# A two-block fp32 model on one core: norm sums and spread at fixed places among the products, weight casts behind that chain, modulation steps behind their place, first weights freed sooner

## The chip, the cores and the metric

The kernel runs on one core of a Trainium2 chip. The metric is the device time of one execution in microseconds; lower is better. The engines are called PE (TensorE, matrix products), DVE (VectorE), ACT (ScalarE), POOL (GpSimd) and SP (SyncE, which issues the DMAs). PEld is PE's own loading of stationary operands, which runs beside its products.

## The reference, cut to what matters

A sequence of 256 tokens `x` and 256 context tokens `ctx`, width 1024, go through a first block of two layers, and `x` then through a second block of two mixers. Only the first block is touched by the change. One of its layers reads, cut:

```
mod = silu(c) @ w_ada[li] + b_ada[li]          # six vectors of 1024: shift, scale, gate, twice
h = rms_norm(x, norm1_w) * (1 + sc1) + sh1
p = h @ w_in[li]                               # attention, a gated recurrence and a Fourier mix follow
x = x + g1 * (concat(att, rec, four) @ w_out[li])
h = rms_norm(x, norm2_w) * (1 + sc2) + sh2
u = conv3(h @ w_up[li])
x = x + g2 * ((silu(gate) * val) @ w_down[li])
# the same for ctx; in the second layer ctx only feeds the keys, the values and the states
```

`rms_norm` divides each token by the root of its mean square, so a layer's first product can't start before the last value of `x` of the step before has been added and squared.

## The kernel before, in words

`x` lies in SBUF as 8 tiles of 128 rows (the width) by 512 columns: columns 0 to 255 are the tokens (v = 0), 256 to 511 the context (v = 1). A product of fp32 operands is made of three: each operand is split into a high part (fp32r) and a low part, and high·high, high·low and low·high are added up in one bank of PSUM. The weights are read from HBM in pieces of 512 KB (`raw`, three buffers, issued by SP); ACT casts the high part `wH` (L136), DVE subtracts it for the low part `wL` (L138); `wH` and `wL` have two buffers each, so a third weight's casts wait until the first one's products are through.

Stages in order, with their place in the span: layer 0 (0 to 353 us, 512 columns, its last 15 us the output products in two halves of 256), its ffn (`w_up` from 356, `w_down` to 765; called FFN0 here), layer 1 (766 to 976, where the context goes only through a part of the products), its ffn (977 to 1185, 256 columns, FFN1), then the second block.

Where one stage follows another stands a **chain**, once for each half v that goes on: the last `add` to `x` (DVE, L733 in a layer, L934 in an ffn); its square on ACT (L200) and the sum `acc` of the squares (L201); `sums`, two products of `acc` with ones (L206); the root on ACT (L212); the reciprocal (L214) and two diagonals `dg` (L223) on DVE; `spread`, two products with ones (L224), which give 1/rms in all rows. Then the modulated input of the next products: for tiles k = 0 and 1 `norm_modulate` (`y` on DVE L422, high part on ACT L423, low part on DVE L424), for k = 2 to 7 `norm` (DVE, L396) and `modulate` (high part ACT L408, `y` POOL L410, low part DVE L411).

A scheduler puts each engine's instructions in order when the kernel is built, by priorities and its own estimate of times; within an engine the order is then fixed, and an instruction that waits holds up all behind it. `urgent` raises a priority; `issue_after(ins)` holds an instruction until `ins` is issued in that estimate. `rstd` is the chain before from sums to spread. `wload(..., hold=...)` holds the casts of a weight's two halves. `gemm` and `gemms` issue the products and count ticks; after so many ticks (`beside`) one step of `ada_steps` is issued: two DMAs of `w_ada` (`araw`, three buffers) and four products (L337) that work out the next modulation vectors, in layer 0 beside the products and in FFN0.

## Time and profile before

| | us |
|---|---|
| median of 3 runs | 1767.48 |
| lowest, highest | 1767.39, 1772.09 |
| the profiled execution's own time | 1768.71 |
| its span in the profile | 1766.8 |
| mean granted clock of TensorE | 0.989 |

The profile shows one execution. A row of a timeline gives the start in us, the busy time in us, engine, line, operation, the tiles out<-in, the shape, the count, and in brackets how long the engine had stood idle before it and who released it. A row of the windows gives the stretch, its length, for each engine its busy time with the count of instructions, then the granted clock of TensorE (1.00 is 2.4 GHz, 0.50 is 1.2 GHz) and the share and rate of the DMA engines. A row of the chain of waits gives start, length and what the end of the stretch stood on at that time.

### The profile page before, as it was taken

The page shows a single profiled execution, that of the slowest core. Times are in us where ns is not written, and L with a number is a line of the kernel's source. Part 1 is how long each engine was busy: PE and PEld are TensorE (multiplying, and loading weights), DVE is VectorE, ACT ScalarE, POOL GpSimd, SP SyncE. Part 2 cuts the span into 40 slices and gives each one's busy share as a digit, 9 for nine tenths or more (in the row PEclk, how much of TensorE's full clock was granted, in tenths as well). Part 3 has the DMA queues.
Part 4 walks back from the last instruction along what each step waited for, and adds up shares of the span by engine and source line. Part 5 has one row for each costly group of instructions (what it writes and reads, how often), then busy time and mean ns, then how long its engine had stood idle before and what let it go on. Part 6 is the DMA issues. An engine that isn't in the chain of part 4 may idle for free.

```text
span 1766.8 us, 29276 instructions
## 1 busy us (share of the span) xinstructions
PE 1703.3 (96%) x11646; PEld 1456.3 (82%) x11646; DVE 1018.9 (58%) x1832; ACT 843.6 (48%) x1476; POOL 312.2 (18%) x402
## 2 busy tenths in 40 slices
PE   6999899999999999989998899999999999999998
PEld 3666676887777777878787899999999999899987
DVE  4445756564433444356866666767666754645656
ACT  3435645453322433334655554665444565555543
POOL 1322210121100011125320210122201202121220
PEclk9999999999999999999999899999999999999999
DMA  9664110334445453223133446555555555444441
GB/s 328 219 202 152 45 54 25 97 129 147 146 162 182 145 189 130 86 72 108 69 97 105 141 155 205 174 175 189 183 180 187 180 179 167 154 139 148 151 144 44
DMA packets 86705, 255.45 MB, mean 145 GB/s; under 512 B 8823, under 2 KB 20471, under 8 KB 86568
## 3 DMA queue, kind: packets, MB, share of 16 engines
q1 hardware_dynamic: 86568, 253.58, 43.4%
q8 instruction: 91, 1.49, 0.3%
q14 instruction: 46, 0.38, 0.1%
HBM read 252.42 MB, written 1.13 MB: 144 GB/s over the span
## 4 chain that ended last, share of the span: by engine, by line
PE 88%; DVE 5%; ACT 4%; issue 1%; DMA 1%; POOL 1%; SPq 0%; ACTq 0%; DVEq 0%; POOLq 0%
PE pg L158 34%; PE ps L158 14%; PE pu L158 7%; PE ph L158 7%; PE pg L184 7%; PE pa L337 3%; PE pg L172 2%; PE ps L1227 2%; PE ph L499 1%; PE ps L172 1%; PE pa L1257 1%; DVE wL L138 1%; PE ps L774 1%; ACT wH L136 1%; PE ph L1253 1%
## 5 line engine op out<-in xcount | busy, mean ns | idle before, releaser
L138 DVE TENSOR_TENSOR wL<-raw,wH 128x1024 fp32r<-128x1024 f32 (+2 forms) x388 | 444.4, 1176 | 219.1 <-ACT wH L136 216.5
L136 ACT CAST wH<-raw 128x1024 fp32r<-128x1024 f32 (+2 forms) x388 | 370.5, 994 | 374.2 <-PE pg L158 149.5
L158 PE MATMUL pg<-hx,wH 128*128 128x256 f32 x1152 | 215.0, 284 | 0.0
L158 PE MATMUL pg<-hm,wH 128*128 128x512 f32 (+1 forms) x672 | 181.1, 356 | 4.6 <-DVE x L733 4.3
L158 PEld LDWEIGHTS pg<-hx,wH 128*128 128x128 f32 x1152 | 178.6, 189 | 5.3 <-issue 4.0
L158 PE MATMUL pg<-hx,wL 128*128 128x256 f32 x576 | 163.1, 283 | 0.0
L158 PEld LDWEIGHTS pg<-hm,wH 128*128 128x128 f32 x672 | 115.8, 190 | 34.6 <-issue 10.2
L926 POOL TENSOR_TENSOR tt<-tt 128x512 f32<-128x512 f32 (+1 forms) x44 | 45.0, 1022 | 451.5 <-DVE tt L923 451.5
L158 PE MATMUL pg<-hm,wL 128*128 128x512 f32 (+1 forms) x336 | 118.4, 352 | 0.0
L158 PEld LDWEIGHTS pg<-hx,wL 128*128 128x128 f32 x576 | 108.2, 188 | 0.7 <-issue 0.2
L158 PE MATMUL pg<-h,wH 128*128 128x512 f32 (+1 forms) x416 | 105.0, 342 | 0.5 <-ACT wH L136 0.5
L158 PE MATMUL ps<-h,wH 128*128 128x512 f32 (+1 forms) x416 | 104.1, 340 | 0.0
L158 PEld LDWEIGHTS pg<-h,wH 128*128 128x128 f32 x416 | 70.7, 190 | 18.4 <-ACT wH L136 8.3
L158 PE MATMUL pg<-hid,wH 128*128 128x256 f32 (+1 forms) x360 | 81.9, 319 | 1.1 <-ACT wH L136 1.1
L158 PEld LDWEIGHTS ps<-h,wH 128*128 128x128 f32 x416 | 71.4, 190 | 10.8 <-ACT bt L974 0.8
L158 PE MATMUL ps<-hid,wH 128*128 128x256 f32 (+1 forms) x344 | 77.8, 319 | 0.0
L184 PE MATMUL pg<-wH,hm 128*128 128x256 f32 x384 | 72.9, 285 | 1.2 <-ACT wH L136 1.2
L201 POOL TENSOR_TENSOR acc<-acc,y 128x256 f32<-128x256 f32 x40 | 36.9, 933 | 197.9 <-ACT y L200 197.3
L158 PEld LDWEIGHTS pg<-hm,wL 128*128 128x128 f32 x336 | 63.8, 190 | 9.7 <-issue 1.0
L158 PE MATMUL ps<-h,wL 128*128 128x512 f32 (+1 forms) x208 | 70.8, 340 | 0.5 <-DVE wL L138 0.5
L158 PE MATMUL pg<-h,wL 128*128 128x512 f32 (+1 forms) x208 | 70.7, 340 | 0.5 <-DVE wL L138 0.5
L184 PE MATMUL pg<-wH,hx 128*128 128x256 f32 x384 | 71.1, 280 | 0.0
(453 smaller groups left out, 3955.0 us busy)
## 6 DMA issues: line engine op xcount, KB each, us to landing
raw<-in_w_up_dram SPq DMA_DIRECT2D x88, 512.0 KB, 4.9
araw<-in_w_ada_dram SPq DMA_DIRECT2D x80, 512.0 KB, 4.6
raw<-in_attn_w_in_dram SPq DMA_DIRECT2D x80, 512.0 KB, 4.6
raw<-in_conv_w_in_dram SPq DMA_DIRECT2D x64, 512.0 KB, 4.6
raw<-in_w_in_dram SPq DMA_DIRECT2D x48, 512.0 KB, 4.7
raw<-in_w_down_dram SPq DMA_DIRECT2D x32, 384.0 KB, 3.7
raw<-in_w_down_dram SPq DMA_DIRECT2D x32, 320.0 KB, 3.1
raw<-in_conv_w_out_dram SPq DMA_DIRECT2D x16, 512.0 KB, 4.6
```

Of the source, the lines that this page charges most:

```text
L136: nc.scalar.copy(H[:, a:b], raw)
L138: nc.vector.tensor_tensor(L[:, a:b], raw, H[:, a:b].bitcast(F32), OP.subtract)
L158: nc.tensor.matmul(pt, a[:, k, c0:c0 + P], c[:, t0:t0 + T], start=n == 0, stop=n == tot - 1)
L172: nc.tensor.matmul(pt, a[:, k, c0:c0 + P], c[:, ts], start=k == 0 and n == 0, stop=k == last and n == 2)
L184: nc.tensor.matmul(pt[:, p0:p0 + 256], c[:, t0:t0 + P], a[:, k, :], start=n == 0, stop=n == tot - 1)
L201: st["last"] = i, (nc.vector if last else nc.gpsimd).tensor_tensor(st["acc"], st["acc"], sq, OP.add)
L337: nc.tensor.matmul(pa[32 * g:32 * g + 32, :], self.csil[:, k, :], raw[g // 2][:, g % 2], start=k == 0, stop=k == KD - 1)
L499: nc.tensor.matmul(pt[:, v, c:c + P], l, m, start=True, stop=True)
L774: nc.tensor.matmul(pts[i][:, :n], qa[h][rr, qt * P:(qt + 1) * P], kT[h][rr, k0 * P:k0 * P + n], start=True, stop=True)
L926: nc.gpsimd.tensor_tensor(tt[1], tt[0], tt[1], OP.mult)
L1227: nc.tensor.matmul(ps[v][:, o:o + ks.stop - ks.start], qh[g][rr[v], i, qs], kh[g][rr[v], i, ks], start=True, stop=True)
L1253: nc.tensor.transpose(pt[:, v, k * P:(k + 1) * P], lts[v][:, k * P:(k + 1) * P], self.ident)
```

## The change

All matrix products go through one function, `product`, which counts them. `in_products(n, f)` calls `f` after n more products. `rstd` is replaced by `chain(st, bank, n)`: it issues the sums after n[0] products and the spread after n[1], each held behind the product before it, and the next product is held behind them. The sums and the spread of one chain now share a bank (columns 256 and 257, and 0 to 255). The places are 20 and 40 products into the second half of `w_out` (for FFN0's v = 1), 12 and 30 products into FFN0's first products (v = 0), 20 and 46 into the last products of `w_down` (layer 1's v = 1), 12 and 30 into layer 1's first (v = 0). At the start of layer 0 and of FFN1 the chain has no number.

The casts of the first weights of layer 1 (`w_in` 8) are held behind the root and the diagonals of v = 1's chain, those of the second (`w_in` 6) behind the high and the low part of v = 0's tile k = 1, those of FFN0's `w_up` 1 (second half) and FFN1's `w_up` 1 (both halves) behind the chain of v = 0. The low parts of k = 6 and 7 of v = 1 are held behind v = 0's diagonals. The products of an `ada` step are held behind the last product issued. The first products of layer 0 now go through k = 0 to 3 for all four groups, then k = 4 to 7 for the first weight's two groups, then for the second's; in layer 1 and in both ffns the first weight's groups come ahead of the second's in the same way. `gemms` counts no ticks any more. `bias_rows` (10 products for the second block) moves from FFN0 to FFN1.

The diff, cut to its core:

```diff
+    def product(self, pt, a, b, start, stop):
+        with self.after(self.first):
+            self.mm = self.nc.tensor.matmul(pt, a, b, start=start, stop=stop)
+        self.first = None
+        self.done += 1
+        while self.plan and self.plan[0][0] <= self.done:
+            self.plan.pop(0)[1]()
+
+    def in_products(self, n, f):
+        self.plan.append((self.done + n, f))
...
-    def rstd(self, st):
-        pn = self.pg()
-        self.sums(pn, 0, st["acc"].rearrange("p (j t) -> p j t", j=2))
-        return self.spread(self.inv("rs", pn[:, 0:2]))
+    def chain(self, st, bank, n=None):
...
+        def sums():
+            st["pt"] = pt = bank()
+            with self.urgent(), self.after(self.mm if n else None):
+                mm = self.sums(pt, 256, st["acc"].rearrange("p (j t) -> p j t", j=2))
+            if n:
+                self.first = mm
+            with self.urgent():
+                st["r"] = self.inv("rs", pt[:, 256:258])
...
+                st["ends"] = self.root, i
...
+        for i, f in enumerate((sums, spread)):
+            if n:
+                self.in_products(n[i], f)
+            else:
+                f()
...
-            for g in range(4):
-                nc.tensor.matmul(pa[32 * g:32 * g + 32, :], self.csil[:, k, :], raw[g // 2][:, g % 2],
-                                 start=k == 0, stop=k == KD - 1)
+            with self.after(self.mm):
+                for g in range(4):
+                    nc.tensor.matmul(pa[32 * g:32 * g + 32, :], self.csil[:, k, :], raw[g // 2][:, g % 2],
+                                     start=k == 0, stop=k == KD - 1)
...
-            first = [(self.wload(d["w_in"][li, 8]),), None]
...
-                if v:
-                    first[1] = (self.wload(d["w_in"][li, 6], hold=((None, None), (None, last))),)
+            self.chain(states[0], lambda: self.psum("pu"), (12, 30))
+            first = [(self.wload(d["w_in"][li, 8], hold=(states[1]["ends"],) * 2),), None]
...
-                self.gemms(groups, acts)
+                if li == 0:
+                    groups = [(first[i // 2][0], i % 2 * P, 0, pts[i]) for i in range(4)]
+                    self.gemms(groups, acts, 0, 4)
+                    self.gemms(groups[:2], acts, 4)
+                    self.gemms(groups[2:], acts, 4)
+                else:
+                    for s in (1, 0):
+                        for k in (0, 4):
+                            modulated(s, k)
+                            if s == k == 0:
+                                w = self.wload(d["w_in"][li, 6], hold=(first[1],) * 2)
...
+            if v:
+                self.chain(st2[1], lambda: self.psum("pa"), (20, 40))
...
+        if ns == 2:
+            self.chain(st2[0], lambda: self.psum("pu"), (12, 30))
...
+            pre.append(self.wload(d["w_up"][li, 1], hold=((None, None), st2[0]["ends"])))
...
+        else:
+            self.chain(st2[0], lambda: self.psum("pu"))
+            pre.append(self.wload(d["w_up"][li, 1], hold=(st2[0]["ends"],) * 2))
...
+                    if v:
+                        self.chain(st1[1], lambda: self.psum("pa"), (20, 46))
```

What it does to the order of the instructions, at three places. The first is PE in layer 0's first products, at k = 4 (`hm_154` and on); before, `pg_472` and `ps_475` are banks of the first and second weight, and the L337 rows are a modulation step:

```order
L172 MATMUL pg_473<-hm_154,wH_237 128x512
L172 MATMUL ps_474<-hm_154,wH_239 128x512
L172 MATMUL ps_475<-hm_154,wH_239 128x512
L337 MATMUL pa_624<-araw_625,csil_77 32x512 x2
L337 MATMUL pa_624<-araw_626,csil_77 32x512 x2
L172 MATMUL pg_472<-hm_155,wH_237 128x512
L172 MATMUL pg_472<-hm_154,wL_238 128x512
```

And now (the banks are `pg_470` to `ps_473`):

```order
L152 MATMUL pg_471<-hm_154,wH_237 128x512
L152 MATMUL ps_472<-hm_154,wH_239 128x512
L152 MATMUL ps_473<-hm_154,wH_239 128x512
L152 MATMUL pg_470<-hm_155,wH_237 128x512
L152 MATMUL pg_470<-hm_154,wL_238 128x512
L152 MATMUL pg_471<-hm_155,wH_237 128x512
```

The step is gone from between the products; the first one now stands some 80 rows later, inside the value products that follow.

The second is PE at the entry to layer 1, from the last product of `w_down` on (`hid`, before):

```order
L158 MATMUL ph_6139<-hid_5687,wL_6016 128x256
L224 MATMUL pg_6217<-dg_6216,ca_71 128x128 x2
L206 MATMUL pg_6222<-ca_71,acc_5740 128x1 x2
L224 MATMUL pg_6230<-dg_6229,ca_71 128x128
L172 MATMUL pg_6331<-hm_6193,wH_6235 128x256
L172 MATMUL pg_6331<-hm_6194,wH_6235 128x256
```

Now the spread of v = 1 (L261) stands among the products of `w_down`:

```order
L152 MATMUL ps_6072<-hid_5659,wH_5976 128x256
L152 MATMUL ps_6072<-hid_5658,wL_5977 128x256
L261 MATMUL pa_6093<-dg_6100,ca_71 128x128 x2
L152 MATMUL pg_6120<-hid_5156,wH_5986 128x256
L152 MATMUL pg_6120<-hid_5155,wL_5987 128x256
```

Before, v = 0's sums and half its spread stood ahead of the first product of layer 1; now they stand behind its first 12 and 30.

The third is DVE at the same entry, from v = 1's reciprocal on; before (`wL_6236` is `w_in` 8, `wL_6284` the first half of `w_in` 6):

```order
L138 TENSOR_TENSOR wL_6236<-raw_6237,wH_6235 128x1024
L138 TENSOR_TENSOR wL_6236<-raw_6241,wH_6235 128x1024
L201 TENSOR_TENSOR acc_5740<-acc_5740,y_6136 128x256
L214 RECIPROCAL rs_6214<-sd_6212 128x2
L223 TENSOR_SCALAR dg_6216<-ca_71,rs_6214 128x128 x2
L934 SCALAR_TENSOR_TENSOR x_80<-ph_6139,mod0_162,x_80 128x256
L422 SCALAR_TENSOR_TENSOR y_6245<-x_80,A1b_5691,pg_6217 128x256
L138 TENSOR_TENSOR wL_6284<-raw_6285,wH_6283 128x1024
L201 TENSOR_TENSOR acc_5740<-acc_5740,y_6174 128x256
L424 SCALAR_TENSOR_TENSOR hm_6194<-y_6245,mod1_3657,hm_6193 128x256
```

and now (`wL_6192` is `w_in` 8):

```order
L226 RECIPROCAL rs_6098<-sd_6096 128x2
L254 TENSOR_SCALAR dg_6100<-ca_71,rs_6098 128x128 x2
L996 SCALAR_TENSOR_TENSOR x_80<-ps_6072,mod0_162,x_80 128x256
L139 TENSOR_TENSOR wL_6192<-raw_6193,wH_6191 128x1024
L139 TENSOR_TENSOR wL_6192<-raw_6197,wH_6191 128x1024
L212 TENSOR_TENSOR acc_5711<-acc_5711,y_6117 128x256
L996 SCALAR_TENSOR_TENSOR x_80<-pg_6120,mod0_162,x_80 128x256
L463 SCALAR_TENSOR_TENSOR y_6205<-x_80,A1b_5662,pa_6093 128x256
```

The two casts of `w_in` 8 have moved from ahead of the reciprocal to behind the diagonals, still ahead of `y`; those of `w_in` 6 (not shown) to behind v = 0's first two low parts.

## Rows read from the trace of the kernel before

**Rows 1.** The page, busy time, share of the span and instructions, PE.

```profile
PE 1703.3 (96%) x11646; PEld 1456.3 (82%) x11646; DVE 1018.9 (58%) x1832; ACT 843.6 (48%) x1476; POOL 312.2 (18%) x402
```

**Rows 2.** Windows: layer 1's entry, FFN1's entry; granted clock behind POOL's column.

```profile
770.00:776.50 6.50, 3.26 (x15) 3.29 (x16) 4.99 (x13) 3.65 (x8) 4.38 (x6) 0.50 0.13 51
...
982.00:988.50 6.50, 5.50 (x25) 5.21 (x25) 4.60 (x10) 3.59 (x8) 4.17 (x6) 0.52 0.04 16
```

**Rows 3.** Timeline of PE, layer 0's first products (columns as told above).

```profile
52.71 3.28 PE L337 MATMUL pa<-araw,csil 128*32 128x512 f32 x8
...
66.60 1.91 PE L337 MATMUL pa<-araw,csil 128*32 128x512 f32 x12
68.44 0.39 PE L184 MATMUL pg<-wH,hm 128*128 128x256 f32 x1
```

**Rows 4.** Timeline of DVE, the casts behind layer 0's first products.

```profile
66.78 2.36 DVE L138 TENSOR_TENSOR wL<-raw,wH 128x1024 fp32r<-128x1024 f32 x2 [0.91 <-ACT wH L136]
```

**Rows 5.** Timeline of ACT: a wait early in layer 0, a table load later.

```profile
27.09 0.37 ACT L372 COPY araw<-pa 128x256 f32<-128x256 f32 x1 [6.42 <-PE pa L317]
...
1190.81 1.28 ACT L1017 ACT_TABLE_LOAD   x1
1192.10 0.20 ACT L1017 ACTIVATE sd<-m 128x2 f32<-128x2 f32 x1
```

**Rows 6.** Timeline of PE, FFN0's entry and its third weight.

```profile
358.68 0.58 PE L172 MATMUL ph<-h,wH 128*128 128x256 f32 x1 [0.89 <-DVE h L424]
...
386.43 0.50 PE L158 MATMUL ps<-h,wL 128*128 128x512 f32 x1 [0.46 <-DVE wL L138]
```

**Rows 7.** The chain of waits through layer 1's entry.

```profile
763.48 4.44 DMA raw<-in_w_in_dram
...
772.67 4.11 POOL y L410 x5
...
777.15 1.22 DVE wL L138
...
781.09 3.67 PE pg L172 x29
```

**Rows 8.** Timeline of ACT, layer 1's entry.

```profile
761.15 2.00 ACT L136 CAST wH<-raw 128x1024 fp32r<-128x1024 f32 x2 [2.55 <-PE pu L158]
...
763.37 0.24 ACT L212 ACTIVATE sd<-pg,eps 128x2 f32<-128x2 f32 x1
```

**Rows 9.** Timeline of PE, layer 1's entry, then its third weight.

```profile
765.42 0.67 PE L224 MATMUL pg<-dg,ca 128*128 128x128 f32 x4
...
773.24 0.77 PE L224 MATMUL pg<-dg,ca 128*128 128x128 f32 x2 [4.44 <-DVE dg L223]
...
796.33 0.38 PE L184 MATMUL pg<-wH,hm 128*128 128x256 f32 x1 [1.17 <-ACT wH L136]
797.59 0.38 PE L184 MATMUL pg<-wL,hm 128*128 128x256 f32 x1 [0.88 <-DVE wL L138]
```

**Rows 10.** Timeline of DVE, layer 1's entry.

```profile
766.12 0.48 DVE L422 SCALAR_TENSOR_TENSOR y<-x,A1b,pg 128x256 f32<-128x256 f32 x1
766.58 1.23 DVE L138 TENSOR_TENSOR wL<-raw,wH 128x1024 fp32r<-128x1024 f32 x1
```

**Rows 11.** Timeline of PE, FFN1's entry and its third weight.

```profile
979.84 1.22 PE L224 MATMUL ps<-dg,ca 128*128 128x128 f32 x4 [1.39 <-DVE dg L223]
...
984.22 0.58 PE L172 MATMUL pg<-h,wH 128*128 128x256 f32 x1 [0.82 <-DVE h L424]
...
997.81 0.50 PE L158 MATMUL pg<-h,wH 128*128 128x256 f32 x2 [0.52 <-ACT wH L136]
999.07 0.38 PE L158 MATMUL pg<-h,wL 128*128 128x256 f32 x1 [0.52 <-DVE wL L138]
```

**Rows 12.** Timeline of DVE, FFN1's entry.

```profile
978.16 1.23 DVE L138 TENSOR_TENSOR wL<-raw,wH 128x1024 fp32r<-128x1024 f32 x1 [0.51 <-ACT wH L136]
...
981.10 0.87 DVE L422 SCALAR_TENSOR_TENSOR y<-x,A,ps 128x256 f32<-128x256 f32 x2 [1.12 <-PE ps L224]
```

More of the change, by code (lines that the diff above doesn't have):

```diff
@@ L64 @@
     rush = True
+    done, mm, plan, first = 0, None, [], None
     def ring(self, tag, shape, dtype=F32):
@@ L157, in gemm @@
             for a, c in ((H, h), (H, l), (L, h)):
-                nc.tensor.matmul(pt, a[:, k, c0:c0 + P], c[:, t0:t0 + T], start=n == 0, stop=n == tot - 1)
+                self.product(pt, a[:, k, c0:c0 + P], c[:, t0:t0 + T], n == 0, n == tot - 1)
                 n += 1
@@ L161, in gemm, with gemms @@
         return pt
-    def gemms(self, groups, acts):
+    def gemms(self, groups, acts, k0=0, k1=KD):
         nc = self.nc
         last = len(acts) - 1
-        for k, (h, l) in enumerate(acts):
+        for k in range(k0, k1):
+            h, l = acts[k]
             for (H, L), c0, t0, pt in groups:
@@ L171, in gemms @@
                 for n, (a, c) in enumerate(((H, h), (H, l), (L, h))):
-                    nc.tensor.matmul(pt, a[:, k, c0:c0 + P], c[:, ts], start=k == 0 and n == 0,
-                                     stop=k == last and n == 2)
-        for _ in groups:
-            self.tick()
+                    self.product(pt, a[:, k, c0:c0 + P], c[:, ts], k == 0 and n == 0, k == last and n == 2)
     def gemm_nat(self, W, acts, t0, pt, p0):
@@ L211, in inv @@
         sd = self.sml("sd", [P, 2])
-        nc.scalar.activation(sd, src, AF.Sqrt, bias=self.eps, scale=1.0 / 1024)
+        self.root = nc.scalar.activation(sd, src, AF.Sqrt, bias=self.eps, scale=1.0 / 1024)
         rs = self.sml(name, [P, 2])
@@ L225, in spread @@
         return pb
-    def rstd(self, st):
-        pn = self.pg()
-        self.sums(pn, 0, st["acc"].rearrange("p (j t) -> p j t", j=2))
-        return self.spread(self.inv("rs", pn[:, 0:2]))
+    def chain(self, st, bank, n=None):
+        nc = self.nc
+        def sums():
[6 more added lines that the diff above has]
+                st["r"] = self.inv("rs", pt[:, 256:258])
+                st["dg"] = dg = self.sml("dg", [P, 2, P], bufs=1)
+                for j in range(2):
+                    i = nc.vector.tensor_scalar(dg[:, j], self.ident, st["r"][:, j:j + 1], None, op0=OP.mult)
+                st["ends"] = self.root, i
+        def spread():
+            st["pb"] = st["pt"][:, 0:256]
+            with self.urgent(), self.after(self.mm if n else None):
+                for j in range(2):
+                    mm = nc.tensor.matmul(st["pb"][:, j * P:(j + 1) * P], self.ones, st["dg"][:, j],
+                                          start=True, stop=True)
+            if n:
+                self.first = mm
+        for i, f in enumerate((sums, spread)):
+            if n:
+                self.in_products(n[i], f)
+            else:
+                f()
     def setup(self, es):
@@ L410, in modulate @@
                 nc.gpsimd.tensor_scalar(y, n[:, i], a, b, op0=OP.mult, op1=OP.add)
-                last = nc.vector.tensor_tensor(L, y, H.bitcast(F32), OP.subtract)
+                with self.after(hold):
+                    last = nc.vector.tensor_tensor(L, y, H.bitcast(F32), OP.subtract)
         return last
@@ L585, in layer @@
                 self.wpart(*w, 4, 8)
-        pb = [None] * 2
-        for v in (1, 0):
-            with self.urgent():
-                pb[v] = self.rstd(states[v])[:, 0:256]
+        if li == 0:
+            self.chain(states[1], lambda: self.psum("pu"))
+            self.chain(states[0], lambda: self.psum2()[:, 0])
         tags = ["on", "on", "aT", "ks", "qh", "sg", "tot"]
```

77 lines of the change are left out of this document (42 added, 35 removed).

## The prediction, made before the changed kernel had run

> **What bounds the kernel now.** I read the page first. PE is busy for 96% of the span, by the profile's modelled ends [rows 1], so almost everywhere the products are the time and no reordering of other engines can gain. What can be gained lies where PE stands. The windows show where: PE is fully packed inside the ffns and the second block, and the loose stretches are the entries from one stage to the next. I then read these on PE, DVE and ACT together, at four places: layer 0's first products, FFN0's entry, layer 1's, FFN1's. Each is followed, some 12 to 30 us later, by a second short stand, the **join**, where the third weight is needed and its casts have only just begun, because the two buffers of weights come free with the last of the first products.
>
> The reader is to see two things. At layer 1's entry PE's queue is the obstacle: v = 0's spread stands in it ahead of the first product of v = 1, and waits 4.44 us for diagonals that DVE makes behind other work [rows 9]. And every stand costs twice, since the granted clock has fallen to 0.50 there, in 770 to 776.5 as in 982 to 988.5 [rows 2]: a 256-column product takes 0.213 us start to start instead of 0.118.
>
> **The change part by part.** Gains are positive.
>
> *Layer 0's first products.* A modulation step of eight rows stands at 52.71 between the products and takes 3.28 us; the twelve at 66.60 take 1.91, 0.159 each [rows 3]. So eight need 1.27, and 2.0 us of the 3.28 is a wait for the step's DMA. The new order has neither piece: the products end 3.28 earlier, at 63.3. The value products then wait for their weight. Its casts begin 3.28 earlier too, and about 0.5 more because the first weight's groups are evicted sooner: the first low part, which started at 66.78 and is half of 2.36 [rows 4], is there at 64.2, and the values start at about 64.4 instead of 68.44 [rows 3], 4.0 earlier. The twenty step rows have still to be done, inside PE's work: 20 × 0.159 = 3.2. If all of it is exposed 0.8 is left; if all falls in waits, 4.0; if one step waits 2.0 for its data again, −1.2. I take **1.4**, near the exposed end, since PE as a whole has only 4% of waits to hide them in [rows 1].
>
> *FFN0's entry.* v = 1's spread now stands 8 products ahead of the end of `w_out`, 0.95 earlier. But on DVE a cast (1.23, the duration in [rows 10]) and two sums of squares now stand ahead of `y`, so `y` comes at about 355.6 and the first low part at 358.2 to 358.6; before, PE ran on from 358.68 [rows 6]. v = 0's sums, until now done while PE stood, move among the products and cost 0.36. Net **0** (−0.5 to 0.9).
>
> *FFN0's join.* The third weight's product at 386.43 waits for a low part [rows 6], 0.86 from the start of the one before it where 0.23 is normal. The first weight's groups now end 24 to 48 products sooner and its buffer with them, so the casts lie beside products: **0.6** (0 to 1.1).
>
> *Layer 1's entry.* Before: ACT's root of v = 1 stood behind two weight casts of 2.00 and ran at 763.37 [rows 8]; the spread ran at 765.42, the first product came behind the two rows of v = 0's spread, at 773.66 [rows 9], then half clock, then a second stand for v = 0, and the last of these products started at 794.89, 1.44 before the 796.33 of [rows 9], and ended at 795.0. Now, walked along the new order: v = 1's sums at 761.1, the root at once, the spread at 762.95, among the products. These end at 765.8, 0.36 later, for v = 1's spread is among them. The casts of `w_in` 8 wait for a buffer until 762.95 and run on ACT to 765.0; their two low parts (2.36, [rows 4]) and two adds stand on DVE ahead of `y`, which comes at 767.5 instead of 766.12 [rows 10]. So this part of the chain gets **later** by 1.4. But PE's queue is free: first product 768.35, first low part 770.2, then one tile per 0.82, POOL's pace (4.11 for five, [rows 7]), so that v = 1's products end at about 778.5. v = 0's spread stands behind the 30th of them, at 776.5; its first low part comes at 780, where PE went on with v = 0 from 781.09 [rows 7]. Behind it the 48 products of v = 0 and the 48 of `w_in` 6 are free to mix: 96 × 0.118 = 11.3, end at 791.3, against 795.0. Gain **3.7**. Bounds: the two low parts of `w_in` 6 now stand on DVE ahead of v = 0's third tile (before, one of them, 1.22, stood at 777.15 ahead of its first [rows 7]); if the mixing doesn't cover them, 1.4 is lost again: 2.3. If the clock is back at full as soon as the low parts flow, 5.5.
>
> *Layer 1's join.* Two stands, 1.44 and 1.26 from start to start before the products at 796.33 and 797.59 [rows 9]; less two products of 0.118, 2.46 lost. Now the groups of `w_in` 8 end 19 products, 2.2 us, before the rest, and the third weight's casts start that much sooner: **1.9** (0 to 2.46).
>
> *FFN1's entry.* One half only, so no numbers: sums at 977.7 as before. The root no longer stands behind two casts, which brings the spread from 979.84 [rows 11] to 979.1. One cast, which stood ahead of the reciprocal at 978.16 [rows 12], now stands ahead of `y`, which comes at 980.75 instead of 981.10; the weight's second cast, 1.2, which came after all low parts, now stands ahead of the first of them. So that low part comes at 984.6 to 984.95, where PE ran on from 984.22 [rows 11]: **−0.7** (−1.5 to 0.8).
>
> *FFN1's join.* Stands of 0.79 and 0.80 before the products at 997.81 and 999.07 [rows 11], 1.35 lost; the first weight's groups end 36 products (4.2 us) sooner: **1.35** (0.7 to 1.35).
>
> *Edits at nothing.* `bias_rows` moves from one packed ffn to another. The same products, squares and casts are issued in all. Two table loads are added on ACT, 1.28 each [rows 5]: the first falls early in layer 0, into a wait of 6.42 us [rows 5], the second into layer 0's attention, where PE's work covers ACT; without that cover 1.3.
>
> On these loads a row and a rule differ: in [rows 5] the load at 1190.81 takes 1.28 and the next activation starts 0.01 us behind it. The Trainium skill, in "ScalarE: Activation LUTs", section "What ACT_TABLE_LOAD costs", adds a drain and comes to about 2.66 us for each switch. By the page an uncovered load would cost 2.66 and the forecast would be 2.66 later than the sum; the row is used.
>
> Sum: 1.4 + 0 + 0.6 + 3.7 + 1.9 − 0.7 + 1.35 = 8.25. The profiled execution took 1768.71, 1.2 above the median; from it 1760.5, and from the median 1767.48 − 8.25 = **1759.2**. A measurement of this kernel tells about 0.3% from no change, which is 5.3 us; 8.25 is above that, by little.
>
> **The rivals.**
>
> *The casts eat it.* For: at all three entries a cast has moved from ahead of the diagonals to between them and the first low part, and DVE, not PE, would then be the bound. Against: at layer 1 PE's own queue waited, and that is gone for certain. With 2.3 at layer 1, −1.5 at FFN1's entry, 1.35 at its join and nothing else, 2.1 is gained: 1765.3.
>
> *The chain does not get shorter at all.* That is, sums and spread are earlier but the first product isn't, because it waits for DVE as before. Then the joins alone pay, 0.6 + 1.9 + 1.35, and layer 0 its 1.4: 5.25, or 1762.2, on the bound of what can be told. Against: the order has the wait of 4.44 out of PE's way.
>
> *All of it comes, and the clock with it.* With shorter stands the granted clock does not fall, or is sooner back: 4.0 + 0.9 + 1.1 + 5.5 + 2.46 + 0.8 + 1.35 = 16.1, 1751.4. Against: at each entry PE still stands for two to three us by my walk, and over stands of such length it fell to 0.50 [rows 2].
>
> *Slower: the pinned steps.* A modulation step is now held behind a given product. PE takes its queue in order, so a step whose `araw` hasn't landed holds up all products behind it, as the one at 52.71 did for 2.0 [rows 3]. Layer 0 has some 15 steps, and SP now issues some of the raw weights ahead of `araw`. Five of them standing 2.0 each eat the gain of 8.25; from seven on (14) the kernel is slower by over 5.3. With ten, 1767.48 − 8.25 + 20 = 1779. Against: one step in this trace stands that long, not several.
>
> **How the numbers follow.** The forecast as walked 0.56, the casts eat it 0.20, only joins 0.06, all of it 0.10, pinned steps 0.08. Faster by over 0.3%: nine tenths of the forecast (its bounds, 4 to 13 gained, reach a little under 5.3), half of the joins alone, and all of it: 0.51 + 0.03 + 0.10 = 0.64. Within 0.3%: 0.05 + 0.20 + 0.03 = 0.28. Slower 0.08. The range leaves out half of the largest gain and the pinned steps with a little of the casts' case: 1752.5 to 1768.
>
> **What would show it.** In the trace after: at layer 1's entry no wait of several us on the spread, a first product near 768.4 and an end of the first products near 791; at the joins of layer 1 and FFN1 stands under 0.5; at FFN1's entry a first low part **later** against the sums than before, by about 0.5; in layer 0 no L377 between the first products. I am wrong if the step rows stand long again, with a wait on the `araw` DMA, or if the first product of layer 1 comes no sooner than the 773.66 of before.

## The result

The changed kernel took 1776.95 us (median of 5 runs, 1772.34 to 1779.82), the kernel before 1767.39 beside it: a ratio of 1.0051, 95% interval 1.0029 to 1.0073. It is slower by about 9 us where 8 us less were forecast. The profiled execution took 1776.95 with a span of 1774.9. The page of the changed kernel, the line that answers to [rows 1]:

```profile
PE 1709.4 (96%) x11646; PEld 1461.2 (82%) x11646; DVE 1019.8 (57%) x1832; ACT 846.7 (48%) x1478; POOL 310.8 (18%) x402
```

The page doesn't say where the time went: the same work, the same shares. A **ledger** does. Both kernels issue the same 9234 products (by `product`, or L158, L172 and L184 before) in nearly the same order. So I numbered them in order of start in each trace and took, for the n-th, its start in one kernel less its start in the other, both counted from the first product. (Before that first product the code is bound by the first DMAs; it came at 31.07 us in the profiled run of before and at 26.9 to 30.6 us in all others, also in b1 below, which is the kernel before up to there. That is run to run and belongs to no edit.) Where the difference changes, a stretch has gained or lost:

| products | stretch | predicted loss | measured loss, us |
|---|---|---|---|
| 0 to 900 | layer 0 | −1.4 | +9.24 |
| 900 to 1100 | FFN0's entry | 0 | +1.42 |
| 1100 to 1300 | its join, and bias_rows gone from there (predicted at 0) | −0.6 | −3.94 |
| 2600 to 2840 | layer 1's entry | −3.7 | −2.16 |
| 2840 to 2858 | its join | −1.9 | −1.52 |
| 3600 to 3756 | FFN1's entry | +0.7 | −0.16 |
| 3756 to 3780 | its join | −1.35 | −1.54 |
| 3855 to 3880 | bias_rows in FFN1 | 0 | +5.04 |
| 5318 to 5500 | start of the second block | 0 | +3.86 |
| all | | −8.25 | +10.35 |

Everywhere else the two run in step to 0.1 us. The six entries and joins on which the change was argued came out within 1.6 us of the prediction each (FFN0's join without `bias_rows`, see the end), and together they gain. Nearly all of the loss lies in three stretches of which the prediction said one gain and two zeros.

A ledger is read from one trace of each kernel, and traces differ. The runs of the experiments below tell by how much: where two of them run the same code with PE's rows in the same order, a difference between them belongs to no edit. The changed kernel, e2 and e3 share layer 0's order and end it at +9.24, +8.47 and +10.37; the seven runs that share e1's end it at −2.74 to −7.18. Between products 96 and 440 the three stand at +8.16 to +8.17 and the seven at −2.88 to −4.14, so that stretch is firm; the rest of layer 0 scatters. Layer 1's entry gains 1.59 to 3.38 in the ten traces that have its code, FFN1's lies between −0.64 and +1.40 in nine. FFN0's first product and the joins of layer 1 and FFN1 agree to 0.03. Where a cause is found for such a difference, below, it is a stretch in which one trace has a granted clock of 0.50 and the other 1.00.

**Layer 0.** PE of the changed kernel, the modulation steps in the value products and scores behind the first products, in order of time:

```profile
70.36 1.07 PE L377 MATMUL pa<-araw,csil 128*32 128x512 f32 x8
74.35 1.05 PE L377 MATMUL pa<-araw,csil 128*32 128x512 f32 x4
77.28 1.05 PE L377 MATMUL pa<-araw,csil 128*32 128x512 f32 x4
...
164.95 1.04 PE L377 MATMUL pa<-araw,csil 128*32 128x512 f32 x2
166.29 1.06 PE L377 MATMUL pa<-araw,csil 128*32 128x512 f32 x6
```

A step is eight rows. A piece of it takes 1.04 to 1.07 us whether it holds 8, 6, 4 or 2 rows, and 1.18 to 1.40 from the last product before it to the first behind it. In the changed kernel nearly every step up to 104 us is cut in two, and each half pays in full: 14 pieces for the first 64 rows, where the kernel before has 9. No piece stands for its DMA. The price was to be read in the kernel before too, where four rows and eight take the same:

```profile
77.12 1.05 PE L337 MATMUL pa<-araw,csil 128*32 128x512 f32 x4
...
81.09 1.07 PE L337 MATMUL pa<-araw,csil 128*32 128x512 f32 x8
```

**bias_rows in FFN1.** PE, then ACT, of the changed kernel, then the window behind the stand:

```profile
1009.45 0.60 PE L1038 MATMUL ps<-bt,rb 33*16 33x256 f32 x2
...
1010.33 0.59 PE L1038 MATMUL pu<-bt,rb 33*16 33x256 f32 x2
...
1011.19 0.59 PE L1038 MATMUL ph<-bt,rb 33*16 33x256 f32 x2
1012.81 0.53 PE L152 MATMUL ps<-h,wH 128*128 128x256 f32 x2 [1.03 <-ACT bt L1039]
```

```profile
1009.44 1.99 ACT L137 CAST wH<-raw 128x1024 fp32r<-128x1024 f32 x2 [1.03 <-PE pg L152]
...
1012.41 0.34 ACT L1039 COPY bt<-ps 16x256 f32<-16x256 f32 x1
```

```profile
1012.40:1016.60 4.20, 3.79 (x19) 3.79 (x20) 2.02 (x5) 1.81 (x7) 0.73 (x1) 0.59 0.78 252
```

Five products take five banks (`ps`, `pg`, `pu`, `ps`, `ph`), and the next product needs one of them back. ACT copies the first only at 1012.41, behind two casts and three other pieces of work. PE stands for 1.03 us, and the granted clock falls to 0.59 over the next 4.2. The loss of 5.04 is made of the stand, the lower clock (by estimate 0.41 of the 4.2 us, 1.7) and the five products themselves (2.26, by e2).

**The start of the second block.** PE and ACT of the changed kernel, then the windows ahead of and from the stand (granted clock behind POOL's column, as in [rows 2]):

```profile
1191.49 0.72 PE L217 MATMUL ph<-ca,acc 128*128 128x1 f32 x6
1192.40 0.28 PE L217 MATMUL ph<-ca,acc 128*128 128x1 f32 x2
1196.70 0.50 PE L152 MATMUL ph<-hx,wH 128*128 128x256 f32 x2 [2.36 <-ACT sd L224]
```

```profile
1192.98 1.99 ACT L137 CAST wH<-raw 128x1024 fp32r<-128x1024 f32 x2 [2.80 <-PE ps L152]
1194.99 1.28 ACT L1082 ACT_TABLE_LOAD   x1
1196.29 0.20 ACT L1082 ACTIVATE sd<-m 128x2 f32<-128x2 f32 x1
1196.40 0.24 ACT L224 ACTIVATE sd<-ph,eps 128x2 f32<-128x2 f32 x1
```

```profile
1190.00:1194.20 4.20, 4.20 (x37) 4.13 (x36) 1.84 (x7) 1.40 (x3) 0.00 (x0) 1.00 0.61 208
1194.20:1202.40 8.20, 5.84 (x37) 5.70 (x36) 2.93 (x6) 2.42 (x4) 0.00 (x0) 0.79 0.37 131
```

The norm sums of the second block now lie in bank `ph`, of which there is one buffer, and the next products want `ph` too. They wait until the root has read the sums, behind two casts and a table load. Before, the sums lay in `ps`, of which there are two, and PE went on without a wait:

```profile
1187.30 0.72 PE L206 MATMUL ps<-ca,acc 128*128 128x1 f32 x6
```

Nothing in the diff names this place: `pg()` deals banks out in turn, the chain no longer calls it and `bias_rows` now calls it later, so the turn arrives shifted.

**The entries.** PE of the changed kernel: FFN0's (answers to [rows 6]), layer 1's with its join ([rows 9]) and FFN1's ([rows 11]):

```profile
364.63 0.58 PE L152 MATMUL pg<-h,wH 128*128 128x256 f32 x1 [4.08 <-ACT h L464]
366.67 0.58 PE L152 MATMUL pg<-h,wH 128*128 128x256 f32 x1 [0.82 <-DVE h L465]
...
767.50 0.61 PE L261 MATMUL pa<-dg,ca 128*128 128x128 f32 x4
772.83 0.47 PE L152 MATMUL pg<-hm,wH 128*128 128x256 f32 x2 [2.36 <-ACT hm L464]
...
798.35 0.38 PE L152 MATMUL pg<-wL,hm 128*128 128x256 f32 x1 [0.77 <-DVE wL L139]
...
981.54 0.58 PE L152 MATMUL pg<-h,wH 128*128 128x256 f32 x1 [1.31 <-ACT h L464]
984.71 0.58 PE L152 MATMUL pg<-h,wH 128*128 128x256 f32 x1 [1.95 <-DVE h L465]
```

The wait of 4.44 us on the spread in [rows 9] is gone, as the change says: neither spread of layer 1 waits (v = 0's follows below). In its place stand waits for the high and low parts.

### The profile page after: what moved, and what is told of

It is laid out like the page before. It is cut to its first block, busy times and chain, and to the rows that moved or that the text cites. A ratio compares the mean times of both kernels' runs of the same rounds, so it can differ in the third digit from the quotient of the medians.

```text
span 1774.9 us, 29276 instructions
## 1 busy us (share of the span) xinstructions
PE 1709.4 (96%) x11646; PEld 1461.2 (82%) x11646; DVE 1019.8 (57%) x1832; ACT 846.7 (48%) x1478; POOL 310.8 (18%) x402
## 4 chain that ended last, share of the span: by engine, by line
PE 89%; ACT 4%; DVE 4%; issue 1%; DMA 1%; POOL 0%; SPq 0%; ACTq 0%; DVEq 0%; POOLq 0%
PE pg L152 43%; PE ps L152 17%; PE pu L152 7%; PE ph L152 7%; PE pa L377 3%; PE ps L1292 2%; PE ph L540 1%; PE ps L828 1%; PE pa L1322 1%; ACT wH L137 1%; PE ph L1318 1%; DVE wL L139 1%; PE pu L866 1%; ACT e L834 1%; PE pa L356 1%
## 5 line engine op out<-in xcount | busy, mean ns | idle before, releaser
L152 PE MATMUL pg<-hm,wH 128*128 128x512 f32 (+1 forms) x768 | 210.2, 357 | 13.1 <-DVE x L785 3.8
L152 PEld LDWEIGHTS pg<-hm,wH 128*128 128x128 f32 x768 | 133.6, 192 | 48.5 <-issue 14.3
L152 PE MATMUL pg<-h,wH 128*128 128x256 f32 (+1 forms) x528 | 132.7, 337 | 8.2 <-ACT h L464 5.4
L152 PE MATMUL pg<-hm,wL 128*128 128x512 f32 (+1 forms) x384 | 134.8, 352 | 0.0
L152 PE MATMUL ps<-h,wH 128*128 128x256 f32 (+1 forms) x512 | 129.5, 338 | 1.0 <-ACT bt L1039 1.0
L152 PEld LDWEIGHTS pg<-h,wH 128*128 128x128 f32 x528 | 92.4, 194 | 19.4 <-ACT h L464 5.9
L152 PEld LDWEIGHTS ps<-h,wH 128*128 128x128 f32 x512 | 89.9, 197 | 20.0 <-ACT wH L137 9.2
L152 PE MATMUL pg<-h,wL 128*128 128x256 f32 (+1 forms) x264 | 88.2, 334 | 0.0
L152 PE MATMUL ps<-h,wL 128*128 128x256 f32 (+1 forms) x256 | 85.6, 335 | 0.0
L152 PEld LDWEIGHTS pg<-hm,wL 128*128 128x128 f32 x384 | 73.9, 192 | 12.4 <-issue 3.2
```

The costliest lines, as they stand in the source:

```text
L152: self.mm = self.nc.tensor.matmul(pt, a, b, start=start, stop=stop)
```

## The experiments

Theory A, formed on the ledger: three separate losses (cut steps, bias_rows' banks, the bank of the second block's sums), and under them a change that gains. The rivals: pinned steps that stand for their DMA, as I had written it; the reordered attention of layer 0; weight casts that are late anyway. The ratio given is to the kernel before, timed beside each batch (medians 1766.34 to 1768.42); ledgers are counted from the first product.

**e1: whole steps.** On the changed kernel:

```diff
-            with self.after(self.mm):
-                for g in range(4):
-                    nc.tensor.matmul(pa[32 * g:32 * g + 32, :], ...)
+            mm = self.mm
+            for g in (2, 0, 1, 3):
+                with self.after(mm):
+                    i = nc.tensor.matmul(pa[32 * g:32 * g + 32, :], ...)
+                if g == 2:
+                    mm = i
```

> The changed kernel with one edit: the four products of a modulation step are held together behind the one that needs the later of the step's two DMAs, so that a step is never cut in two. Theory A (a piece of a step costs PE 1.19 to 1.3 us whether it holds 2, 4 or 8 rows, since its products lie side by side in the array; the change cut the steps of the first 107 us into 14 pieces where the kernel before had 9): layer 0 has 16 pieces in place of 25, and the ledger of product starts shows 5 to 9 us less by the end of layer 0; total 1768 to 1772. Rival B (pinned steps stand for their araw DMA): a step held for its second DMA waits longer, the rows of a step span over 1.5 us each, and the total is no better than 1775. Rival C (the loss is the reordered attention from 164 us on): the ledger at product 300 stays at +5 and only noise moves.

Measured 1765.89 us, ratio 0.9987 (0.9972 to 1.0003), 11 us under the changed kernel. Layer 0 ends at −5.26 against the kernel before, where the changed kernel had +9.24. Its steps, PE:

```profile
74.81 1.06 PE L378 MATMUL pa<-araw,csil 128*32 128x512 f32 x8 [0.21 <-DMA araw<-in_w_ada_dram]
80.68 1.07 PE L378 MATMUL pa<-araw,csil 128*32 128x512 f32 x8
```

Two of the first seven wait for their DMA, by 0.21 and 0.16 us, so rival B falls, and rival C with it: by product 300 the ledger is at −2.63. 14.5 us came back where nine pieces at 1.2 make 10.8. Of the 14.5, 1.6 lie ahead of product 96, where PE's order is the same and traces scatter, 12.2 between products 96 and 440, and 0.7 behind. The seven runs with these whole steps take 11.0 to 12.3 less between 96 and 440 than the three with cut ones. The order changes there along with the pieces, so the two aren't fully apart in this run.

**e2: bias_rows back in FFN0.**

```diff
-                if li == 1 and j == 4:
+                if li == 0 and j == 4:
                     self.bias_rows()
+                if li == 1 and j == 4:
+                    self.gi += 5
...
+            self.gi -= 5
             st = self.ffn(1, st, 256)
```

> The changed kernel with bias_rows back in the first ffn (bank rotation of the second ffn and the second block kept as in the changed kernel). Theory A (in the second ffn five banks of bias rows hold up the next products until ACT has copied them, behind two casts, and the clock falls): the loss of 5.0 us between products 3855 and 3880 goes, the first ffn pays about 3.2 again: 1.8 us less in all, about 1775. Rival B (the second ffn loses there anyway because its weights' casts are late): the stand of 1.4 us stays and the total rises by 3.

Measured 1771.02, ratio 1.0024 (1.0012 to 1.0036). Between products 3855 and 3880 the loss is 0.00 in place of 5.04, and FFN0 pays 2.26 of its 3.2 again: 2.8 less from the two places. A further 1.5 came off the second block's start, though its banks are as in the changed kernel. The stand is there as well, but in this trace the granted clock stays at 1.00, where the changed kernel has 0.79 in the window shown above:

```profile
1191.56 0.50 PE L152 MATMUL ph<-hx,wH 128*128 128x256 f32 x2 [2.35 <-ACT sd L224]
```

```profile
1187.20:1195.40 8.20, 5.84 (x49) 5.64 (x49) 3.37 (x8) 3.63 (x5) 0.00 (x0) 1.00 0.40 141
```

So of the 3.86 there, 2.36 are the wait and 1.5 the clock, and these 1.5 belong to no edit of e2. Why the clock fell in one and not in the other is open. The median is 5.9 lower than the changed kernel's, but the intervals of the two ratios meet; the account goes by the ledger.

**e3: the turn of the banks.**

```diff
+            self.gi += 4
             self.block2(st[0])
```

> The changed kernel with the rotation of PSUM banks moved on by four at the start of the second block, so that its norm sums lie in ps, of which there are two, as in the kernel before, and no longer in ph, of which there is one. Theory A (the next products wait for ph until the root has read the sums, behind two casts and a table load, and the clock falls): the stand of 2.64 us at 1194 and the half-clock stretch behind it go, 3.5 to 3.9 us less, about 1773. Rival B (the stand is that of the casts of the next weight): it stays at 2 us or more in another bank, and the total is the same within 1.

Measured 1770.77, ratio 1.0022 (1.0008 to 1.0036); from product 5318 to 5500 the loss is 0.00 in place of 3.86. PE at this place:

```profile
1193.51 0.72 PE L217 MATMUL ps<-ca,acc 128*128 128x1 f32 x6
1194.41 0.28 PE L217 MATMUL ps<-ca,acc 128*128 128x1 f32 x2
1201.47 0.61 PE L236 MATMUL pu<-dg,ca 128*128 128x128 f32 x4
```

No wait is left between the sums and the spread. Theory A holds, rival B falls.

**e4: the three together.**

> The three edits together on the changed kernel. Theory A (three separate losses): they add up, 5 to 9 + 1.8 + 3.5 to 3.9 us less than the changed kernel, 1762 to 1767, so at or below the kernel before. Rival B (the losses hide behind one another, or layer 0's is the DMA): 1770 or more.

Measured 1757.74 (1754.55 to 1761.84), ratio 0.9947 (0.9929 to 0.9965): 19 us under the changed kernel and 10.7 under the kernel before. That is more than theory A's 1762 to 1767, and rival B falls. By the ledger it ends at −10.41; what the edits mend in the changed kernel's ledger is 20.8, of which layer 0 is 12.9.

**b1: whole steps on the kernel before.** The edit of e1 there (without `self.mm`).

> The kernel before with the one edit of e1: modulation steps kept whole. Theory A (each piece costs PE 1.2 to 1.3 us, in the kernel before as well, which has 23 pieces in layer 0 where 16 steps stand): 7 pieces less, 5 to 9 us, 1760 to 1763, by the end of layer 0. Then the cut steps are no fault of the change alone, and the change with its three losses mended is worth only the rest of e4's gain, 2 to 5 us. Rival B (the order of the kernel before hides its pieces in waits): the same as the kernel before within 2.

Measured 1766.55, ratio 1.0005 (0.9994 to 1.0015): no difference. Theory A's total is wrong, and the ledger says why. From 23 pieces to 16 it gains 5.48 by product 440, as expected; between products 440 and 600, in the attention, it loses 5.78 again. There PE stands twice between 184 and 188 us, 1.37 and 1.54, around the transposes of the finished modulation vectors, which now follow later steps, and the granted clock is at 0.52 from 186 to 193. So the cost of a cut is real in the kernel before too, but the order that the scheduler finds behind it decides whether it is kept.

**e9: the hold on the steps undone,** on the changed kernel (the only run that undoes a line of the diff in layer 0):

```diff
-            with self.after(self.mm):
-                for g in range(4):
+            for g in range(4):
```

> The changed kernel with one line undone: the products of a modulation step are no longer held behind the last product issued. The order then has 23 pieces in layer 0, at the same places as in the kernel before, one of them the step between layer 0's first products. Theory A (layer 0's loss of the changed kernel is the holding of the steps, which cuts them into 25 pieces with 14 of them ahead of the first attention): counted from layer 0's first product to the end of layer 0 the kernel takes 5 to 9 us less than the changed one, and what is left is what the second block's start and bias_rows cost. Rival B (the other edits of layer 0, the order of its first groups and of the banks, lose the time): no less than 2 us of the 9 comes back.

Measured 1770.89, ratio 1.0019 (1.0010 to 1.0028). Layer 0 ends at +2.67 in place of +9.24: 6.6 us of its loss are the hold, within theory A's 5 to 9; between products 96 and 440 alone it is 8.2 (−0.05 in place of +8.17). Of the 2.67, 1.06 have come by the end of the first products, whose order is new. Another 1.55 come between products 540 and 560, where PE's order is that of the kernel before: e9 runs them from 200.6 to 204.0 us at a granted clock of 0.51, the kernel before at 1.00. So the clock makes this part, not the order. What is left of the total, +4.08, is the 2.67, FFN0's entry (2.5), bias_rows and the second block's start, less the gains at the other entries and the joins.

**e10: a piece measured by itself.** e4, with each of FFN0's 24 steps cut in two:

```diff
+            if li == 1:
+                part((2, 3))
+                self.in_products(12, lambda part=part: part((0, 1)))
+            else:
+                part((2, 0, 1, 3))
```

> A direct measure of a piece: e4 with each of the 24 modulation steps beside the first ffn's products cut in two, two of its four products 12 products later; nothing else changes, and PE is packed there. Theory A (a piece costs 1.2 us of PE whatever it holds): 24 x 1.2 = 29 us more than e4, all between products 1150 and 2400. Rival B (the cost goes with the rows, 0.159 each): 0 to 3 us more.

A single run: 1786.31 us. The ledger against e4 grows by 28.0 us between products 1160 and 2400, in jumps of 1.17 to 1.19 for each added piece; 24 × 1.2 = 28.8. Elsewhere it moves by less than 2 us either way, as between other traces of one order. PE, e10 and then e4 at the same work:

```profile
393.53 1.05 PE L379 MATMUL pa<-araw,csil 128*32 128x512 f32 x4
...
397.51 1.05 PE L379 MATMUL pa<-araw,csil 128*32 128x512 f32 x4
```

```profile
390.59 1.06 PE L378 MATMUL pa<-araw,csil 128*32 128x512 f32 x8
```

This settles the price: a piece costs 1.2 us of packed PE, and its rows cost next to nothing (1.05 for four, 1.06 for eight).

**e5 and e6: casts behind the chain for good.** In e4, FFN0's second weight with both halves held, and FFN1's second half held behind the second low part:

```diff
-            pre.append(self.wload(..., hold=((None, None), st2[0]["ends"])))
+            pre.append(self.wload(..., hold=(st2[0]["ends"],) * 2))
```

```diff
-            pre.append(self.wload(..., hold=(st2[0]["ends"],) * 2))
-            modulated(0)
+            modulated(0, 0, 2)
+            pre.append(self.wload(..., hold=(st2[0]["ends"], self.nm)))
+            modulated(0, 2)
```

> e4 with one edit: the first half of the second weight of the first ffn, whose casts e4 lets run ahead of y, is held behind the diagonals of v = 0 as well. Theory A (that low-part cast of 1.23 stands on DVE between the last sums and y, and y is what PE waits for): the first ffn's first product and first low part come 1.0 to 1.2 sooner against the last product of layer 0 than in e4, and it stays so to the end of those products: about 1.1 less in all. Rival B (another cast or the low parts' pace takes its place, or the casts are late for the second weight's products): 0 within 0.3, or a new stand of a us before the second weight's first product.

> e4 with one edit: in the second ffn the second half of the second weight is cast behind the first two low parts, no longer ahead of them. Theory A (this cast of 1.21 on DVE is what the first low part waits for, the loss that was predicted there): the first low part comes 1.2 sooner, the third 0.4 to 0.8 later; 0.4 to 0.9 less at the end of these products. Rival B (POOL's pace, 0.82 a tile, sets the end of these products whatever the first low part does): the end of these products moves by less than 0.3.

e5: 1757.60, ratio 0.9952 (0.9935 to 0.9969); e6: 1755.08, ratio 0.9940 (0.9922 to 0.9958). In time neither can be told from e4, in the ledger e5 can. From product 900 to 960, FFN0's first, e4 loses 1.30 (nine traces with this entry 1.28 to 1.31) and e5 gains 0.82, 2.1 us better, more than theory A's 1.0 to 1.2; but it doesn't stay so, by product 1100 the difference is 0.78. From 3660 to 3756 e4 loses 0.69 (nine traces 0.46 to 1.04) and e6 gains 0.08: 0.77 by these two; with e8, which has the same edit and loses 0.41, it may be less. PE at FFN1's entry, e6 and then e4:

```profile
969.81 0.58 PE L152 MATMUL pg<-h,wH 128*128 128x256 f32 x1 [1.31 <-ACT h L467]
971.84 0.58 PE L152 MATMUL pg<-h,wH 128*128 128x256 f32 x1 [0.81 <-DVE h L468]
```

```profile
969.91 0.58 PE L152 MATMUL pg<-h,wH 128*128 128x256 f32 x1 [1.32 <-ACT h L467]
973.09 0.58 PE L152 MATMUL pg<-h,wH 128*128 128x256 f32 x1 [1.95 <-DVE h L468]
```

The wait for the first low part is 1.14 shorter in e6 without the cast of 1.21 ahead of it: what stands on DVE between `y` and the low part is what PE waits for.

**e7: v = 1's spread as late as before.** In e4, `(20, 46)` becomes `(20, 66)`.

> e4 with one edit: at the entry to layer 1 the spread of v = 1 stands behind all 66 last products of w_down, where the kernel before had it, in place of behind the 46th. Theory A (y waits for casts and adds on DVE, not for the spread, so this place is worth nothing; what gained was to take v = 0's sums and spread out of PE's way): the first product of layer 1 moves by less than 0.4 and the total by less than 0.5. Rival B (the early place of the spread is the gain, as the change's words say): 2 us or more are lost at layer 1's entry.

Measured 1757.40, ratio 0.9961 (0.9937 to 0.9985). From product 2600 to 2840 e7 gains 1.39 where e4 gains 1.60. The first product comes 0.9 later than in e4, counted from product 2600, more than theory A allowed, but at the end of these products 0.2 is left of it. The ten traces with the early place gain 1.59 to 3.38 there, 2.45 in the mean, and e7's 1.39 lies below them all. So the early place of this spread is worth between 0.2 and 2.0 us, by the mean about 1: more than theory A's next to nothing, less than rival B's 2 or more. The 1.39 that e7 keeps can't be its gain; that they come from v = 0's part having left PE's way is argued from the order, and no run undoes that part alone.

**e8: e4 with e5 and e6.**

> e4 with the two edits of e5 and e6 together (both ffns' second weight cast later). Theory A: they add up, 0.8 less each at the ends of those products, 1755 to 1757, about 11 us under the kernel before. Rival B (they only move the stands to the third weights): the same as e4.

Measured 1756.14 (1754.37 to 1764.99), ratio 0.9944 (0.9927 to 0.9961), and a ledger of −10.53: inside theory A's range, and no better than e4. e5's gain is there (0.75 lost from product 900 to 1100 where e4 loses 1.70), but from 3600 to 3756 it loses 1.20 where e4 gains 0.64, and 0.6 more at the second block's start, as e6 does. All of the 1.84 between the two comes by product 3660, ahead of FFN1's first, in rows whose order is the same in both; e6, with the same edit, gains 1.17 there as e4 gains 1.33. e8's granted clock is at 0.50 from 959 to 976 us there, e4's only from 966.6 to 976.9. So that loss tells nothing of the edits, and whether they add up isn't shown. e4, e5, e6 and e8 can't be told apart in time, all about 10 us under the kernel before.

## Why the prediction was wrong, point by point

*Layer 0's first products, "0.159 each".* This is the step that failed. I divided the twelve rows of [rows 3] by their 1.91 us and priced a step by its rows. The price is by piece, 1.2 us (e10), which the same trace showed in the rows at 77.12 and 81.09; the twelve are a piece of eight and one of four behind it. I had put the moved work at 3.2 for twenty rows wherever they go; it went from 2 places into 4 pieces, 4.8. The bulk is what the sum has at nothing: the hold cut the steps behind them as well. Term: +1.4 predicted, −9.24 measured, of which 6.6 is the hold (e9). Of the other 2.67, 1.06 comes in the first products, where ten traces of one order differ by 1.8, and 1.55 is the lower clock of e9's trace in the attention.

*"2.0 us of the 3.28 is a wait for the step's DMA."* The other half of the same term, and a misreading. The row of 3.28 in [rows 3] has no idle time in it; its two halves were two pieces, and from 53.0 on they ran at a granted clock of 0.50. The window of the kernel before, then the same step in e9, at 1.00:

```profile
53.00:56.40 3.40, 3.40 (x9) 0.67 (x6) 1.87 (x5) 2.77 (x5) 3.40 (x5) 0.50 0.90 347
```

```profile
52.16 1.05 PE L376 MATMUL pa<-araw,csil 128*32 128x512 f32 x4
53.64 1.05 PE L376 MATMUL pa<-araw,csil 128*32 128x512 f32 x4 [0.42 <-DMA araw<-in_w_ada_dram]
```

What shows there as a wait for the DMA is 0.42. In the changed kernel, without the step, PE waited 0.53 for a low part at 51.68 and ran at 0.50 from 51.7 to 57.4: the first products end 0.41 later than before, counted from the first product, where 3.28 sooner was predicted (−1.20 to +0.62 in the ten traces), and the value products start 1.5 sooner (1.3 to 3.1) in place of 4.0.

*The rival "pinned steps".* It named the right line of the diff and a wrong mechanism: no step stood 2 us for its DMA, not even the one at 52.71 from which the 2.0 was taken. I gave the slower side 0.08 on that mechanism alone and had not looked at what the hold does to the order: the halves in place of steps in the new order were there to be read.

*"bias_rows moves from one packed ffn to another", at nothing.* FFN0 gained 3.24 where it stood and FFN1 lost 5.04. Of the 3.24, e2 pays 2.26 again; the other 0.98 is a piece of four step rows, which in the kernel before stood by itself behind the five products, at 411.34. I had called both ffns packed, but not counted that the five banks come free only by ACT, nor that ACT there has the casts of a weight every 5.7 us (48 products of 0.118) in place of every 11. The cost of the move is 2.8 net.

*The second block, not looked at.* 3.86, 2.36 of it a wait and 1.5 the clock that fell behind it in this trace (e2), by a turn of banks that the diff never mentions. The order shows the new bank in one row (`ph` for `ps`); I saw that row and took it for nothing.

*FFN0's entry, 0 (−0.5 to 0.9).* −1.42. The walk was right in what stands ahead of `y`, and short on it. DVE of the changed kernel:

```profile
361.56 1.23 DVE L139 TENSOR_TENSOR wL<-raw,wH 128x1024 fp32r<-128x1024 f32 x1 [0.48 <-ACT wH L137]
362.70 0.95 DVE L212 TENSOR_TENSOR acc<-acc,y 128x256 f32<-128x256 f32 x2
363.56 0.87 DVE L463 SCALAR_TENSOR_TENSOR y<-x,A,pa 128x256 f32<-128x256 f32 x2
```

Product 959 lies 7.57 later in this run than in the one of before; by that my 355.6 for `y` is 363.2, and it ran at 363.56. The first low part followed with the product at 366.67, 0.42 later than before by the same count. The rest is a term I left out. v = 1's spread too now takes PE's time among products, where it ran while PE stood: 0.61 is lost by product 959. And v = 0's sums, which I had priced at 0.36, take 0.86 at half clock; with its spread (0.44) that is 1.30 among the first products, where before the spread alone took 0.69. e5 gives 0.78 of the whole back.

*Layer 1's entry, 3.7 (2.3 to 5.5).* 2.16, just under the lower bound (1.59 to 3.38 in the ten traces). PE's wait of 4.44 [rows 9] went, and `y` came later by the casts ahead of it, as written. The products of `w_down` ahead of v = 1's spread, which the walk counts itself, lie 4.45 later in this run; by that my walk's first product at 768.35, first low part at 770.2, spread of v = 0 at 776.5, its first low part at 780 and end at 791.3 are 772.8, 774.65, 780.95, 784.45 and 795.75. Measured: 772.83, 774.88, 781.99, 785.75 and 797.2. So the walk held up to the first low part. Behind it I had left out v = 0's sums: they stand among v = 1's products at half clock and take 0.7, which with the 0.2 ahead of them makes the spread 1.0 late. Then PE waits 0.56 for a cast of `w_in` 6 on ACT and twice for v = 0's low parts, 0.20 and 0.28, as the last rows show (the two casts of `w_in` 6 stand ahead of the last on DVE, which was the lower bound's reason):

```profile
777.18 0.85 PE L217 MATMUL pu<-ca,acc 128*128 128x1 f32 x4
...
781.99 0.61 PE L261 MATMUL pu<-dg,ca 128*128 128x128 f32 x4
...
785.05 0.50 PE L152 MATMUL ps<-hm,wH 128*128 128x256 f32 x2 [0.56 <-ACT wH L137]
785.75 0.39 PE L152 MATMUL pg<-hm,wH 128*128 128x256 f32 x1 [0.20 <-DVE hm L465]
...
789.14 0.39 PE L152 MATMUL pg<-hm,wH 128*128 128x256 f32 x1 [0.28 <-DVE hm L452]
```

DVE shows that there is more to be had here: the diagonals were ready at 779.28, and `y` then waited 2.40 for a spread that PE had behind other products. An earlier place for it was not run.

```profile
778.78 0.50 DVE L254 TENSOR_SCALAR dg<-ca,rs 128x128 f32<-128x128 f32 x2
...
782.63 0.87 DVE L463 SCALAR_TENSOR_TENSOR y<-x,A1b,pu 128x256 f32<-128x256 f32 x2 [2.40 <-PE pu L261]
```

*The joins* (0.6, 1.9, 1.35): 0.7 (3.94 less bias_rows' 3.24), 1.52 and 1.54. Right: freeing the first weight sooner is the part of the change that pays as argued, and the last two gain the same to 0.03 in every trace that has it. *FFN1's entry, −0.7 (−1.5 to 0.8)*: +0.16, inside its bounds, with a sign that one trace can't tell (nine lie between 0.64 gained and 1.40 lost). The mechanism is the one given: the first low part comes 0.7 later against the sums than before, and the cast ahead of it is what it waits for (e6).

*The two table loads*, where the 2.66 of the Trainium skill, "ScalarE: Activation LUTs", section "What ACT_TABLE_LOAD costs", was set against the row's 1.28: the load at 1194.99 again ends at 1196.27 and the activation behind it starts at 1196.29, so the row's price holds in this run too, and the 2.66 doesn't show. What the second added load costs in layer 0's attention was not measured by itself.

Without the three losses the change is worth about what it was argued to be, for another sum: e4's ledger has −3.66 in layer 0 (whole steps), nothing at FFN0, −3.12 at layer 1's entry and join, −1.44 behind them, −2.18 at FFN1's entry and join. The −1.44 are luck: the changed kernel, with the same code there, has +0.11. The kernel before has a granted clock of 0.72 from 936 to 942 us in its trace, e4 at the same products 1.00.

## What to carry to other kernels

Before pricing an operation by its rows, look in the trace for the same operation with fewer of them: if 2, 4 and 8 cost the same, the price is for the piece, and the question to put to a new order is how often it is cut. A hold, or an edit that changes how often a helper deals out buffers, acts on places that the diff doesn't name; compare the order of the whole program, and look at which buffer each waiting instruction gets. And when a total is not what was forecast, number the instructions that both kernels share and subtract their starts: here the three losses came from one table. Take a second trace of the same order beside it, for a stretch of lower clock in one of them moves an entry by 1 to 2 us. A row that is long without idle time in it has not waited: look at the granted clock over it first.

## What the runs showed of the hardware that was not expected

Four fp32 products of 32 output rows each, into four different parts of one bank, cost no more than one, as if they ran side by side: the trace starts the rows of a pair some 7 ns apart, a group of 2, 4, 6 or 8 rows (two rows are one product) took 1.04 to 1.07 us of the profile's busy time and some 1.2 us of the products around it, and 24 more groups of four rows cost 28 us (e10). Behind the stand of 1.03 us in FFN1 the granted clock was at 0.59 over 4.2 us; over 8.2 us with the stand of 2.36 in the second block it was at 0.79 in the changed kernel, a loss of 3.86, and at 1.00 in e2, with the same stand, a loss of 2.36. So the same wait costs more or less by what the clock does behind it, and one trace doesn't tell which.
